# Attention by token tiles of eight heads, two tiles ahead, the product with the values 512 columns wide; the column of a mask constant inside an older tile

## The chip, the cores and the metric

The kernel runs on one core of a Trainium2 chip (trn2). The time is the device time of one execution in microseconds. The core has a matrix engine (TensorE, PE in the profile, with its weight loads as PEld), a vector engine (VectorE, DVE), a scalar engine for activations and copies (ScalarE, ACT), a general engine (GpSimd, POOL) and a sync engine that starts most transfers (SyncE, SP). They run side by side, each through its own queue of instructions in a fixed order, and wait for one another by semaphores. On-chip memory has 128 partitions; results of matmuls land in PSUM, which has eight banks of 2 KB for each partition.

## The reference

One decoder block over 1024 tokens of width 1024, all in float32. What matters here is the attention: eight query heads of 64, two key/value heads, each token sees itself and the 127 tokens before it, and each head has a sink in its softmax.

```python
h = _rmsnorm(x, g_mix_pre[l])
proj = jnp.einsum('bsd,de->bse', h, w_in[l]) + b_in[l]
u_pool, q, k, v, gates = jnp.split(proj, IN_SPLITS, axis=-1)
...
q = _partial_rotary(q.reshape(B, S, N_Q_HEADS, HEAD_DIM), cos, sin)
k = _partial_rotary(k.reshape(B, S, N_KV_HEADS, HEAD_DIM), cos, sin)
...
# in _sliding_window_sink_attention, over blocks of 128 tokens and the block before each
s = jnp.einsum('bnqhgd,bnkhd->bnhgqk', qb, kk).astype(jnp.float32) * scale
rel = qi + BLOCK - kj
band = (rel >= 0) & (rel < WINDOW)
s = jnp.where(valid[None, :, None, None], s, NEG_INF)
p = jax.nn.softmax(jnp.concatenate([s, sink], axis=-1), axis=-1)[..., :-1]
o = jnp.einsum('bnhgqk,bnkhd->bnqhgd', p.astype(v.dtype), vv)
```

Beside it stands a multi-scale pooling branch on the first 512 columns of `proj` (window sums of 2, 4, 8 and 16 tokens, less the token itself). Gates, an output projection and an MLP follow.

## The kernel before

Every matmul operand is split into a high part of reduced precision and a low part, what is left of it (`split`: ACT copies the high part, L103, DVE subtracts, L106). A product is then three matmuls: high by high, high by low, low by high (`PASSES`).

The stages are: projections of queries, keys and values of the first four token tiles while weights and input arrive; the attention stage; the pooling branch and the gates; the merge of both branches; the MLP. The change lies in the attention stage, from about 54 to 180 us of the profile. The stages behind it have the same instructions in the same order before and after.

In the attention stage the order of TensorE's instructions is written out by hand (`tc.manual_schedule` for PE). The order on the other engines is set by the scheduler of the language. Two streams are interleaved on TensorE:

- `others()`, a generator of filling work: the query products (`mm_q`, L182, 512 columns) and key/value products (`mm_kv`, L191, 256 columns) of tiles 4 to 7, each followed by `pre_qkv(n)`, and then the products of the pooling branch's input for its four groups (L533), each scaled by DVE (L536). `fill(t)` takes about t microseconds of it by a planned cost of each piece.
- attention itself, by half-tiles (n, g): token tile n of 128 queries, and four of its eight heads, a group g.

The steps of attention:

- `pre_qkv(n)`: DVE takes queries, keys and values from PSUM, scales them and adds the bias (L261, L262); POOL (DVE for tile 0) rotates.
- `post_qkv(n)`: TensorE transposes queries and keys (L279, L280), ACT and DVE split them into `qt`, `khi` and `klo`; POOL prepares the values `v` and the difference `dv` to the tile before (L286 to L296).
- `score(n, g)`: twelve matmuls (L321) into `sc`, which has a single buffer of two PSUM banks; ACT copies the own block to `s4` (L324); DVE overwrites by a mask with scores of the block before (`copy_predicated`, L326), then the maximum (L329) and the softmax bias (L330). After masking each query has 128 scores in one row: the own block up to the diagonal and the block before past it.
- `attend_t(n, g)`: the sink term (L340, L341), four exponentials with their sums on ACT (L344), sum, reciprocal and scaling on DVE (L345 to L347), four transposes on TensorE (L350) into an `at` bank, the split, and for n > 0 a masked copy of both parts, `pc` (L357).
- `attend_v(n, g)`: the product with the values, matmuls of 256 columns (L367), twelve for a half-tile and six for those of tile 0; ACT copies the result to `y` (L370).

In the loop over the 16 half-tiles, `attend_t` of one half-tile, a fill of 1.6, the score three half-tiles ahead, `post_qkv` two tiles ahead in every other step, a fill of 2.2, and `attend_v` follow each other. Once four tiles are done, SP sends `y` to memory (L579), and its place serves the window sums of `pool_in` (L595, L598) on DVE. These are followed by `pool_mix` (L611 to L613, L614) and the gates (L458).

PSUM is used as: `sc` one buffer of two banks, `at` three banks, `mm` three banks. The buffers named below are in the pool `ap`: `qkv` 4 of 4 KB for each partition, `sc4` 4 of 2 KB, `s4` 4 of 4 KB.

Of the kernel before, what the change touches and what calls it, by code (L numbers as in the profile page):

```python
# [14 lines left out]
P = 128  # L15
# [11 lines left out]
F = 4096  # L27
NF = F // P
HEAD_ORDER = (0, 4, 1, 5, 2, 6, 3, 7)

SOFT_ORDER = (0, 1, 4, 5, 2, 3, 6, 7)


PASSES = ((0, 0), (0, 1), (1, 0))
# [18 lines left out]
def block_kernel(ctx: ExitStack, tc, xt, x, consts, vecs, sinks, b_qkv, g_post, g_mlp, g_mlp_post,  # L53
# [100 lines left out]
    eps = cp.tile([P, 1], F32, name="eps")  # L154
    dve.memset(eps, EPS)
    pad = sp.tile([P, 32], F32, name="pad", bufs=1)
    dve.memset(pad, 0.0)
    warm = small(1, "warm")
    act.activation(warm, eps, AF.Identity)
    ident = cst[:, C_ID:C_ID + P]  # L160
# [1 line left out]

    from_prev = cst[:, C_MASK:C_MASK + P].bitcast(mybir.dt.uint32)
    own_t = cst[:, C_MASK + P:C_MASK + 2 * P]
    neg = cp.tile([P, 1], F32, name="neg")
    dve.memset(neg, NEG)

    def bcast(src, n):
        t = bcp.tile([P, 1024], F32, tag="bc", name=nm("bc"))
# [29 lines left out]
    sq = at("qkv", 4, [S])  # L199
    ones = vec[:, V_ONE:V_ONE + 1]  # L200
    for k in range(NK):
        xs = at("s4", 4, [S])
# [51 lines left out]
    tfs = {}  # L254

    def pre_qkv(n):
        tf = y[1][n - 2].rearrange("p a b -> p (a b)") if n in (2, 3) else at("qkv", 4, [1024])
        tfs[n] = tf
        t = tf[:, :768].rearrange("p (h d) -> p h d", d=HD)
        rn = r1[:, n:n + 1]  # L260
        dve.scalar_tensor_tensor(tf[:, :512], bq[n], rn, bq_b[:, :512], ALU.mult, ALU.add)  # L261
        dve.scalar_tensor_tensor(tf[:, 512:768], bkv_of(n), rn, bq_b[:, 512:768], ALU.mult, ALU.add)  # L262
        c = cst[:, C_COS + 8 * n:C_COS + 8 * n + 8].unsqueeze(1).unsqueeze(1).broadcast_to([P, 10, 2, 8])
        s = cst[:, C_SIN + 8 * n:C_SIN + 8 * n + 8].unsqueeze(1).unsqueeze(1).broadcast_to([P, 10, 2, 8])
        rot = t[:, :10, :ROT].rearrange("p h (a b) -> p h a b", a=2)
# [6 lines left out]
        eng.tensor_tensor(rot[:, :, 1, :], a[:, :, 1, :], b[:, :, 0, :], ALU.add)  # L272

    def post_qkv(n):
        tf = tfs[n]
# [9 lines left out]
        vt = at("v", 4, [2, 3, HD], F32R)  # L285
        pool.memset(f32(vt[:, :, 1, :]), 0.0)  # L286
        split(vt[:, 0, ::2, :], vt[:, 1, ::2, :], t[:, 10:12, :], pool, pool)
        vs[n] = vt.rearrange("p l a d -> p l (a d)")
        qts[n] = qt
        if n:  # L290

            dt_ = at("dv", 3, [2, 3, HD], F32R)
            dv = tf[:, 768:896].rearrange("p (a d) -> p a d", d=HD)
            pool.tensor_tensor(dv, t[:, 10:12, :], tfs.pop(n - 1)[:, 640:768].rearrange("p (a d) -> p a d", d=HD),
                               ALU.subtract)
            pool.memset(f32(dt_[:, :, 1, :]), 0.0)  # L296
            split(dt_[:, 0, ::2, :], dt_[:, 1, ::2, :], dv, pool, pool)
            dvs[n] = dt_.rearrange("p l a d -> p l (a d)")

    scores, soft = {}, {}  # L300

    SCALE = HD ** -0.5

    def score(n, g):


        qt = qts[n]
        k0 = max(n - 1, 0) * P
        nk = 2 * P if n else P
        s4 = at("sc4", 4, [4, P])  # L310
        if g == 0:
            soft[n] = tuple(sp.tile([P, NH], F32, tag=t, name=nm(t)) for t in ("nmx", "es", "den"))
        nmx = soft[n][0]
        sb = bank("sc", [2, 2, 256])

        for i in range(2):
            m = 2 * g + i
            for j, (qx, kx) in enumerate(((0, klo), (1, khi), (0, khi))):
                for kv in range(2):
                    r = slice(kv * HD, (kv + 1) * HD)  # L320
                    pe.matmul(sb[:, kv, i, :nk], qt[r, qx, m * P:(m + 1) * P], kx[r, k0:k0 + nk],  # L321
                              start=j == 0, stop=j == 2)
        heads = sb.rearrange("p a b k -> p (a b) k")
        act.copy(s4, heads[:, :, nk - P:nk])  # L324
        prev = heads[:, :, :P] if n else neg.unsqueeze(1).broadcast_to([P, 4, P])
        dve.copy_predicated(s4, from_prev.unsqueeze(1).broadcast_to([P, 4, P]), prev)  # L326

        gs = slice(4 * g, 4 * g + 4)
        dve.tensor_reduce(nmx[:, gs], s4, AX.X, ALU.max)  # L329
        dve.scalar_tensor_tensor(nmx[:, gs], nmx[:, gs], -SCALE, nsnk[:, gs], ALU.mult, ALU.min)  # L330
        scores[n, g] = s4

    probs = {}

    def attend_t(n, g):

        s4 = scores.pop((n, g))
        nmx, es, den = soft[n]
        gs = slice(4 * g, 4 * g + 4)
        dve.tensor_tensor(es[:, gs], snk[:, gs], nmx[:, gs], ALU.add)  # L340
        act.activation(es[:, gs], es[:, gs], AF.Exp)  # L341
        for j in range(4):
            h = 4 * g + j
            act.activation(s4[:, j], s4[:, j], AF.Exp, scale=SCALE, bias=nmx[:, h:h + 1], accum_out=den[:, h:h + 1])  # L344
        dve.tensor_tensor(den[:, gs], den[:, gs], es[:, gs], ALU.add)  # L345
        dve.reciprocal(den[:, gs], den[:, gs])
        dve.tensor_tensor(s4, s4, den[:, gs].unsqueeze(2).broadcast_to([P, 4, P]), ALU.mult)  # L347
        b = bank("at", [4, P])
        for j in range(4):
            pe.transpose(b[:, j], s4[:, j], ident)  # L350
        pt = at("s4", 4, [2, 4, P], F32R)
        split(pt[:, 0], pt[:, 1], b)
# [7 lines left out]
    def attend_v(n, g):  # L360
        pt, pc = probs.pop((n, g))
        yb = bank("at", [2, P])
        parts = ((vs[n - 1], pt), (dvs[n], pc)) if n else ((vs[0], pt),)
        mms = [(v, p, kv, j) for v, p in parts for kv in range(2) for j in PASSES]
        mms.sort(key=lambda e: (e[1] is pc, e[3][1]))
        for j, (v, p, kv, (vh, ph)) in enumerate(mms):
            pe.matmul(yb.rearrange("p m q -> p (m q)"), v[:, vh, kv * HD:kv * HD + P],  # L367
                      p[:, ph, 2 * kv:2 * kv + 2].rearrange("p i q -> p (i q)"), start=j == 0, stop=j == len(mms) - 1)
# [139 lines left out]
        return ga_.tile([P] + shape, F32R, tag="ga", name=nm("ar"))  # L508

    def others():  # L510
        for n in range(4, NT):
            bq[n] = bank("mm")
            for k in range(NK):
                mm_q(n, k, bq[n])
                yield 3 * 0.227
            if n == NT - 1:
                wu[3] = load_w(w_u[3], [NK, P])
            bkv[n] = bank("at" if n == 4 else "mm", [1, 256])
            for k in range(NK):
                mm_kv(n, k)  # L520
                yield 3 * 0.12
            pre_qkv(n)
        for gi in (3, 2, 1, 0):
            if gi:
                wu[gi - 1] = load_w(w_u[gi - 1], [NK, P])
# [23 lines left out]
                return  # L549
            owed[0] -= c  # L550

    half_steps = [(n, g) for n in range(NT) for g in range(2)]
    with tc.manual_schedule(engines={mybir.EngineType.PE}):
        pre_qkv(0)
        pre_qkv(1)
        pre_qkv(2)
        pre_qkv(3)
# [639 lines left out]
def _layout(inputs):  # L1197
# [18 lines left out]
    for col, t in ((C_COS, np.cos(ang)), (C_SIN, np.sin(ang))):  # L1216
# [48 lines left out]
```

## Time and profile before

| What | Value |
|---|---|
| median of 3 runs | 1159.61 us (1158.52 to 1160.14) |
| the profiled execution, its time | 1159.59 us |
| its span in the profile | 1157.8 us |
| busy PE, DVE, ACT, POOL, 54 to 180 us | 123.27, 107.68, 70.40, 23.72 us of 126 |
| last product with the values begins | 176.71 us |
| first gate matmul begins | 184.09 us |
| mean granted clock of TensorE | 0.993 |

The profile is one execution. The span reaches from the first to the last recorded instruction; the time holds the 1.8 us around it as well. An instruction's length in a timeline is its own; instructions that follow each other without a wait overlap a little, so that the distance between two starts is shorter (a sum over 512 columns on DVE is 0.69 long and its successor starts 0.60 later). The granted clock is the share of full speed that TensorE was given.

### The profile page before, as it was taken

The page shows a single profiled execution, that of the slowest core. Times are in us where ns is not written, and L with a number is a line of the kernel's source. Part 1 is how long each engine was busy: PE and PEld are TensorE (multiplying, and loading weights), DVE is VectorE, ACT ScalarE, POOL GpSimd, SP SyncE. Part 2 cuts the span into 40 slices and gives each one's busy share as a digit, 9 for nine tenths or more (in the row PEclk, how much of TensorE's full clock was granted, in tenths as well). Part 3 has the DMA queues.
Part 4 walks back from the last instruction along what each step waited for, and adds up shares of the span by engine and source line. Part 5 has one row for each costly group of instructions (what it writes and reads, how often), then busy time and mean ns, then how long its engine had stood idle before and what let it go on. Part 6 is the DMA issues. An engine that isn't in the chain of part 4 may idle for free.

```text
span 1157.8 us, 14205 instructions
## 1 busy us (share of the span) xinstructions
PE 1135.5 (98%) x5292; PEld 932.2 (81%) x5292; DVE 825.8 (71%) x1272; ACT 526.1 (45%) x920; POOL 62.9 (5%) x102
## 2 busy tenths in 40 slices
PE   7999999899999999999999999999999999999997
PEld 6888887788888888888788888888888888888885
DVE  7678997987654584766997766666547945446887
ACT  6455547443431334365654444444444345344342
POOL 3522100000000150000000000000000000000000
PEclk9999998999999999999999999999999999999999
DMA  7202107553345453433265434343688665432662
GB/s 253 81 1 64 56 19 273 177 169 128 143 171 179 149 177 109 134 131 119 91 218 218 156 144 160 141 159 141 249 286 301 211 214 170 132 101 73 201 198 92
DMA packets 66165, 179.08 MB, mean 155 GB/s; under 512 B 6192, under 2 KB 6192, under 8 KB 66096
## 3 DMA queue, kind: packets, MB, share of 16 engines
q1 hardware_dynamic: 60336, 157.73, 40.3%
q10 hardware_dynamic: 5760, 20.45, 4.4%
q8 instruction: 41, 0.67, 0.2%
q14 instruction: 28, 0.23, 0.1%
HBM read 127.82 MB, written 50.33 MB: 154 GB/s over the span
## 4 chain that ended last, share of the span: by engine, by line
PE 85%; DVE 9%; ACT 3%; issue 2%; DMA 1%; SPq 0%; DVEq 0%; ACTq 0%
PE mm L458 22%; PE at L458 16%; PE at L1103 14%; PE mm L1103 11%; PE mm L820 7%; PE mm L395 5%; PE mm L397 3%; PE mm L182 2%; PE mm L533 1%; PE at L820 1%; DVE s L357 1%; DVE wh L106 1%; DVE T L106 1%; DVE t L595 1%; DVE s L106 1%
## 5 line engine op out<-in xcount | busy, mean ns | idle before, releaser
L1103 PE MATMUL at<-ar,wh 128*128 128x512 f32 x744 | 169.6, 389 | 0.0
L1103 PEld LDWEIGHTS at<-ar,wh 128*128 128x128 f32 x744 | 139.6, 188 | 29.4 <-DVE ar L106 0.4
L1103 PE MATMUL mm<-ar,wh 128*128 128x512 f32 x576 | 131.0, 389 | 0.0
L1103 PEld LDWEIGHTS mm<-ar,wh 128*128 128x128 f32 x576 | 108.1, 188 | 22.4
L103 ACT CAST wh<-st 128x512 fp32r<-128x512 f32 (+1 forms) x106 | 66.9, 641 | 126.5 <-PE mm L395 36.6
L106 DVE TENSOR_TENSOR wh<-raw,wh 128x1024 fp32r<-128x1024 f32 x53 | 64.8, 1223 | 81.9 <-ACT wh L103 81.8
L103 ACT CAST wh<-raw 128x1024 fp32r<-128x1024 f32 x53 | 55.8, 1053 | 132.8 <-PE at L1103 63.6
L106 DVE TENSOR_TENSOR wh<-st,wh 128x512 fp32r<-128x512 f32 (+1 forms) x106 | 82.9, 788 | 17.9 <-ACT wh L103 15.7
L458 PE MATMUL mm<-gr,wh 128*128 128x512 f32 x300 | 72.7, 392 | 0.1
L458 PE MATMUL mm<-T,wx 128*128 128x512 f32 x288 | 68.0, 391 | 0.0
L458 PEld LDWEIGHTS mm<-gr,wh 128*128 128x128 f32 x300 | 56.0, 188 | 12.3 <-ACT g L885 0.5
L458 PEld LDWEIGHTS mm<-T,wx 128*128 128x128 f32 x288 | 54.1, 188 | 11.7
L458 PE MATMUL at<-T,wx 128*128 128x512 f32 x252 | 59.5, 391 | 0.0
L458 PE MATMUL mm<-x,wh 128*128 128x512 f32 x216 | 55.7, 415 | 3.4 <-ACT g L465 3.4
L458 PEld LDWEIGHTS at<-T,wx 128*128 128x128 f32 x252 | 47.3, 188 | 10.2
L458 PEld LDWEIGHTS mm<-x,wh 128*128 128x128 f32 x216 | 43.2, 200 | 14.5 <-ACT g L465 3.8
L106 DVE TENSOR_TENSOR ar<-B,ar 128x1024 fp32r<-128x1024 f32 x37 | 45.1, 1218 | 8.9 <-ACT ar L103 8.9
L533 PE MATMUL mm<-x,wh 128*128 128x512 f32 x192 | 49.9, 404 | 0.0
L458 PE MATMUL at<-gr,wh 128*128 128x512 f32 x183 | 44.5, 390 | 0.0
L103 ACT CAST ar<-B 128x1024 fp32r<-128x1024 f32 x37 | 38.7, 1046 | 10.7 <-DMA B<-in_w_dn_dram 6.1
L737 DVE TENSOR_TENSOR g<-g,mm 128x512 f32<-128x512 f32 x32 | 20.5, 683 | 31.2 <-PE mm L397 31.1
L533 PEld LDWEIGHTS mm<-x,wh 128*128 128x128 f32 x192 | 34.5, 188 | 7.4
(356 smaller groups left out, 2231.1 us busy)
## 6 DMA issues: line engine op xcount, KB each, us to landing
raw<-f_dram SPq DMA_DIRECT2D x53, 512.0 KB, 3.7
f_dram<-g SPq DMA_DIRECT2D x30, 512.0 KB, 3.2
B<-in_w_dn_dram SPq DMA_DIRECT2D x24, 512.0 KB, 6.1
st<-in_w_up_dram SPq DMA_DIRECT2D x22, 512.0 KB, 3.7
f_dram<-g ACTq DMA_DIRECT2D x17, 512.0 KB, 2.6
st<-in_w_g_dram SPq DMA_DIRECT2D x16, 512.0 KB, 3.7
g<-spill_dram SPq DMA_DIRECT2D x16, 512.0 KB, 4.5
raw<-in_w_dn_dram SPq DMA_DIRECT2D x16, 512.0 KB, 4.6
```

What stands on the lines that cost most here:

```text
L103: act.copy(hi, src)
L106: eng.tensor_tensor(lo, src, f32(hi), ALU.subtract)
L182: pe.matmul(bq, xs_[k][n // 4][:, xh, n % 4 * P:(n % 4 + 1) * P], wq[k][:, h, :], start=k == 0 and j == 0, stop=k == NK - 1 and j == 2)
L357: dve.tensor_tensor(pc[:, h], f32(pt[:, h]), own_t.unsqueeze(1).broadcast_to([P, 4, P]), ALU.mult)
L395: pe.matmul(bs[th], whi[:, k, :], rhs(k, hl, th), start=k == 0 and hl == 0, stop=False)
L397: pe.matmul(bs[th], wlo[:, k, :], rhs(k, 0, th), start=False, stop=k == nk - 1)
L458: pe.matmul(b, w[:, wh, kt, :], xo[kt][:, xh, :], start=not after and kt == 0 and j == 0, stop=kt == 3 and j == 2, skip_group_check=after)
L533: pe.matmul(b, (whi, wlo)[h][:, k, :], xr(k, xh, th), start=k == 0 and j == 0, stop=k == NK - 1 and j == 2)
L595: dve.tensor_tensor(t[:, step:], src[:, step:], src[:, :S - step], ALU.add)
L737: dve.tensor_tensor(z[:, sl], z[:, sl], bs[th], ALU.mult)
L820: pe.matmul(obs[n][dj], l, wos[k][whl][:, dj * 512:(dj + 1) * 512], start=k == 0 and hl == 0 and whl == 0, stop=k == NK - 1 and hl == 1)
L1103: pe.matmul(bs[t], fo[fh][:, k2, t * P:(t + 1) * P], wo_[wh][:, k2, :], start=not after and s2 == 0 and k2 == 0 and j == 0, stop=s2 == NS ...
```

## The change

Attention is done by whole tiles of eight heads.

- Both scores of a tile write halves of one buffer `s8` (three buffers of 4 KB). Maximum, softmax bias, sink term, sum, reciprocal and scaling are done once for eight heads, in a new function `softmax(n)`, which is called right after the tile's second score, two tiles ahead of its use.
- `attend_t(n)` is now the transposes of eight heads into two `at` banks, their splits, and the masked copies at width 1024. The high and low parts are separate `s4` tiles, so that one token tile takes all four buffers.
- `attend_v(n)` makes matmuls of 512 columns, twelve for a tile and six for tile 0, into one bank; ACT copies it in two pieces.
- The loop runs over eight tiles. The fills are 2.5, 2.0 and 2.5, with the two scores of tile n + 2 on either side of the middle one, and `post_qkv` three tiles ahead.
- The filling work makes both query products of tiles 6 and 7 before their key/value products.
- `post_qkv` first copies the values to a tile of their own (`vf`) on POOL; `qkv` has three buffers rather than four.
- The constant for masked scores, `neg`, is a column of the padding tile `pad`, which is now filled with it.
- The sinks are in the order of heads, as the softmax now is.

```diff
-    dve.memset(pad, 0.0)
+    dve.memset(pad, NEG)
...
-    neg = cp.tile([P, 1], F32, name="neg")
-    dve.memset(neg, NEG)
+    neg = pad[:, :1]
...
-        tf = y[1][n - 2].rearrange("p a b -> p (a b)") if n in (2, 3) else at("qkv", 4, [1024])
+        tf = y[1][n - 2].rearrange("p a b -> p (a b)") if n in (2, 3) else at("qkv", 3, [1024])
...
+    def split_v(src, tag, bufs):
+        t = at(tag, bufs, [2, 3, HD], F32R)
+        pool.memset(f32(t[:, :, 1, :]), 0.0)
+        split(t[:, 0, ::2, :], t[:, 1, ::2, :], src, pool, pool)
+        return t.rearrange("p l a d -> p l (a d)")
...
+        vf = at("vf", 3, [2, HD])
+        pool.tensor_copy(vf, t[:, 10:12, :])
+        vfs[n] = vf
+        vs[n] = split_v(vf, "v", 4)
         if n:
-
-            dt_ = at("dv", 3, [2, 3, HD], F32R)
...
+            dv = at("df", 1, [2, HD])
+            pool.tensor_tensor(dv, vf, vfs.pop(n - 1), ALU.subtract)
+            dvs[n] = split_v(dv, "dv", 3)
...
-        s4 = at("sc4", 4, [4, P])
         if g == 0:
-            soft[n] = tuple(sp.tile([P, NH], F32, tag=t, name=nm(t)) for t in ("nmx", "es", "den"))
-        nmx = soft[n][0]
+            scores[n] = at("s8", 3, [2, 4, P])
+        s4 = scores[n][:, :, 2 * g:2 * g + 2, :]
         sb = bank("sc", [2, 2, 256])
...
+        act.copy(s4, sb[:, :, :, nk - P:nk])
+        dve.copy_predicated(s4, wide(from_prev), sb[:, :, :, :P] if n else wide(neg))
+
+    soft = {}
+
+    def softmax(n):
+
+        s8 = scores[n].rearrange("p a b k -> p (a b) k")
+        nmx, es, den = (sp.tile([P, NH], F32, tag=t, name=nm(t)) for t in ("nmx", "es", "den"))
+
+        dve.tensor_reduce(nmx, s8, AX.X, ALU.max)
+        dve.scalar_tensor_tensor(nmx, nmx, -SCALE, nsnk, ALU.mult, ALU.min)
+        dve.tensor_tensor(es, snk, nmx, ALU.add)
+        act.activation(es, es, AF.Exp)
+        for h in range(NH):
+            act.activation(s8[:, h], s8[:, h], AF.Exp, scale=SCALE, bias=nmx[:, h:h + 1], accum_out=den[:, h:h + 1])
+        dve.tensor_tensor(den, den, es, ALU.add)
+        dve.reciprocal(den, den)
+        dve.tensor_tensor(s8, s8, den.unsqueeze(2).broadcast_to([P, NH, P]), ALU.mult)
...
+    def attend_t(n):
+
+        s8 = scores.pop(n)
+        pt = [at("s4", 4, [NH, P], F32R) for _ in range(2)]
+        for kv in range(2):
+            b = bank("at", [4, P])
+            for m in range(4):
+                pe.transpose(b[:, m], s8[:, kv, m], ident)
+            split(*(t[:, 4 * kv:4 * kv + 4] for t in pt), b)
         pc = None
         if n:
-            pc = at("s4", 4, [2, 4, P], F32R)
-            for h in range(2):
-                dve.tensor_tensor(pc[:, h], f32(pt[:, h]), own_t.unsqueeze(1).broadcast_to([P, 4, P]), ALU.mult)
-        probs[n, g] = pt, pc
+            pc = [at("s4", 4, [NH, P], F32R) for _ in range(2)]
+            for t, s in zip(pc, pt):
+                dve.tensor_tensor(t, f32(s), own_t.unsqueeze(1).broadcast_to([P, NH, P]), ALU.mult)
+        probs[n] = pt, pc
+
+    def attend_v(n):
+        pt, pc = probs.pop(n)
+        yb = bank("at", [4, P])
+        mms = [(v, p, kv, j) for v, p in (((vs[n - 1], pt), (dvs[n], pc)) if n else ((vs[0], pt),))
+               for j in ((0, 0), (1, 0), (0, 1)) for kv in range(2)]
         for j, (v, p, kv, (vh, ph)) in enumerate(mms):
             pe.matmul(yb.rearrange("p m q -> p (m q)"), v[:, vh, kv * HD:kv * HD + P],
-                      p[:, ph, 2 * kv:2 * kv + 2].rearrange("p i q -> p (i q)"), start=j == 0, stop=j == len(mms) - 1)
+                      p[ph][:, 4 * kv:4 * kv + 4].rearrange("p i q -> p (i q)"), start=j == 0, stop=j == len(mms) - 1)
         c = (n % 4) * P
-        act.copy(y[n // 4][g][:, :, c:c + P], yb)
+        for g in range(2):
+            act.copy(y[n // 4][g][:, :, c:c + P], yb[:, 2 * g:2 * g + 2])
...
     def others():
-        for n in range(4, NT):
-            bq[n] = bank("mm")
...
+        for qs, kvs in (((4,), (4,)), ((5,), (5,)), ((6, 7), (6, 7))):
+            for n in qs:
+                bq[n] = bank("mm")
...
         fill(8.3)
         post_qkv(0)
         make_rb()
         score(0, 0)
-        fill(2.0)
+        fill(2.5)
         post_qkv(1)
         score(0, 1)
-        fill(4.0)
+        softmax(0)
+        fill(3.0)
         score(1, 0)
-        fill(3.0)
-        for i, (n, g) in enumerate(half_steps):
-            attend_t(n, g)
-            fill(1.6)
-            if i + 3 < len(half_steps):
-                score(*half_steps[i + 3])
-            if g == 0 and n + 2 < NT:
-                post_qkv(n + 2)
-            fill(2.2)
-            attend_v(n, g)
-            if n % 4 == 3 and g == 1:
+        fill(2.5)
+        post_qkv(2)
+        score(1, 1)
+        softmax(1)
+        fill(5.5)
+        for n in range(NT):
+            attend_t(n)
+            fill(2.5)
+            if n + 2 < NT:
+                score(n + 2, 0)
+            fill(2.0)
+            if n + 2 < NT:
+                score(n + 2, 1)
+                softmax(n + 2)
+            if n + 3 < NT:
+                post_qkv(n + 3)
+            fill(2.5)
+            attend_v(n)
+            if n % 4 == 3:
...
-        ("sinks", c(a["attn_sinks"][0][list(SOFT_ORDER)])),
+        ("sinks", c(a["attn_sinks"][0])),
```

More of the change, by code (lines that the diff above doesn't have):

```diff
@@ L198, in block_kernel @@
     bss = bank("at", [NT])
-    sq = at("qkv", 4, [S])
+    sq = at("qkv", 3, [S])
     ones = vec[:, V_ONE:V_ONE + 1]
@@ L272, in pre_qkv @@
         eng.tensor_tensor(rot[:, :, 1, :], a[:, :, 1, :], b[:, :, 0, :], ALU.add)
+    vfs = {}
+    def split_v(src, tag, bufs):
[3 more added lines that the diff above has]
+        return t.rearrange("p l a d -> p l (a d)")
     def post_qkv(n):
-        tf = tfs[n]
+        tf = tfs.pop(n)
         t = tf[:, :768].rearrange("p (h d) -> p h d", d=HD)
@@ L284, in post_qkv, with wide @@
         split(khi[:, ks], klo[:, ks], bk[:, :P])
[L285 to L288, printed above, removed]
         qts[n] = qt
+        vf = at("vf", 3, [2, HD])
+        pool.tensor_copy(vf, t[:, 10:12, :])
+        vfs[n] = vf
+        vs[n] = split_v(vf, "v", 4)
         if n:
-            dt_ = at("dv", 3, [2, 3, HD], F32R)
[L293 to L300, printed above, removed]
+            dv = at("df", 1, [2, HD])
+            pool.tensor_tensor(dv, vf, vfs.pop(n - 1), ALU.subtract)
+            dvs[n] = split_v(dv, "dv", 3)
+    scores = {}
     SCALE = HD ** -0.5
+    def wide(ap):
+        return ap.unsqueeze(1).unsqueeze(1).broadcast_to([P, 2, 2, P])
     def score(n, g):
@@ L322, in score @@
                               start=j == 0, stop=j == 2)
[L323 to L330, printed above, removed]
@@ L331, in score @@
-        scores[n, g] = s4
-    probs = {}
[L335 to L352, printed above, removed]
+        act.copy(s4, sb[:, :, :, nk - P:nk])
@@ L358, in attend_t @@
-        probs[n, g] = pt, pc
[L360 to L365, printed above, removed]
+            pc = [at("s4", 4, [NH, P], F32R) for _ in range(2)]
+            for t, s in zip(pc, pt):
+                dve.tensor_tensor(t, f32(s), own_t.unsqueeze(1).broadcast_to([P, NH, P]), ALU.mult)
@@ L510, in others @@
     def others():
-        for n in range(4, NT):
-            bq[n] = bank("mm")
-            for k in range(NK):
-                mm_q(n, k, bq[n])
-                yield 3 * 0.227
+        for qs, kvs in (((4,), (4,)), ((5,), (5,)), ((6, 7), (6, 7))):
+            for n in qs:
+                bq[n] = bank("mm")
+                for k in range(NK):
+                    mm_q(n, k, bq[n])
+                    yield 3 * 0.227
             if n == NT - 1:
                 wu[3] = load_w(w_u[3], [NK, P])
[L518 to L522, printed above, removed]
+            for n in kvs:
+                bkv[n] = bank("at" if n == 4 else "mm", [1, 256])
+                for k in range(NK):
+                    mm_kv(n, k)
+                    yield 3 * 0.12
+                pre_qkv(n)
         for gi in (3, 2, 1, 0):
@@ L550, in fill @@
             owed[0] -= c
-    half_steps = [(n, g) for n in range(NT) for g in range(2)]
     with tc.manual_schedule(engines={mybir.EngineType.PE}):
[L554 to L557, printed above, removed]
+        for n in range(4):
+            pre_qkv(n)
         fill(8.3)
```

1 line of the change is left out of this document (removed).

## The prediction

> **What bounds the kernel now.** I read the page first: the span, the busy shares and the chain that ended last.
>
> ```profile
> span 1157.8 us, 14205 instructions
> PE 1135.5 (98%) x5292; PEld 932.2 (81%) x5292; DVE 825.8 (71%) x1272; ACT 526.1 (45%) x920; POOL 62.9 (5%) x102
> ...
> PE 85%; DVE 9%; ACT 3%; issue 2%; DMA 1%; SPq 0%; DVEq 0%; ACTq 0%
> ```
>
> TensorE carries 85% of the chain: time is gained or lost where it stands still or runs at a lower clock. Then busy time by stage (columns: stretch, its length, busy us and instructions of PE, PEld, DVE, ACT, POOL, granted clock, DMA share, GB/s). The attention stage, which the change rewrites, is the second row.
>
> ```profile
> 40.00:54.00 14.00, 13.86 (x78) 11.96 (x77) 8.18 (x20) 4.10 (x5) 5.68 (x15) 0.88 0.11 40
> 54.00:180.00 126.00, 123.27 (x831) 104.29 (x829) 107.68 (x229) 70.40 (x229) 23.72 (x59) 1.00 0.14 46
> 180.00:240.00 60.00, 55.22 (x217) 43.77 (x218) 51.03 (x80) 35.90 (x55) 0.00 (x0) 0.91 0.60 208
> ```
>
> In attention PE is busy for 123.3 of 126 us, DVE for 107.7. Then what PE waited for from 54 to 184 us (in total, times, longest):
>
> ```profile
> PE at L611 <- ACT ar L103: 1.9, 1, 1.9
> PE at L350 <- DVE qt L106: 1.1, 2, 0.9
> PE sc L321 <- DVE klo L106: 0.6, 1, 0.6
> PE at L612 <- DVE ar L106: 0.6, 1, 0.6
> ```
>
> Only 1.7 us of PE waits lie inside attention (L350, L321); the other two come after it. Last, PE's timeline at the stage's end:
>
> ```profile
> 176.71 0.88 PE L367 MATMUL at<-s,dv 128*128 128x256 f32 x6
> 177.43 0.40 PE L611 MATMUL at<-ar,wpt 128*128 128x512 f32 x1
> ...
> 180.85 0.79 PE L611 MATMUL at<-ar,wpt 128*128 128x512 f32 x2 [1.87 <-ACT ar L103]
> 182.22 0.79 PE L612 MATMUL at<-ar,wpt 128*128 128x512 f32 x1 [0.57 <-DVE ar L106]
> ...
> 184.09 7.62 PE L458 MATMUL mm<-x,wh 128*128 128x512 f32 x24
> ```
>
> Attention ends at 177.4, the gates begin at 184.1. After a gap of 1.87 and one of 0.57 us the 24 matmuls take 7.46 us start to start (184.09 to 191.55), where 24 at full clock take 5.5 (0.229 each, from nine at 0.228 to eighteen at 0.238). The granted clock reads 0.50 from 182 to 188 us.
>
> **The change, part by part.** It keeps all matmul work but for the product with the values.
>
> *PE.* 180 matmuls of 256 columns become 90 of 512. Six of 256 follow each other in 0.715 us (88.20 to 88.91), 0.119 each: 21.4 us. A 512 takes 0.229: 90 make 20.6. Gain 0.85. Each tile now has one run of transposes and one of the product instead of two; with the boundaries of such runs costing 0.1 to 0.2 (nine matmuls before a score 2.27, before a product 2.18, alone 2.06) that is about 1.0 over eight tiles. If nothing waits, the 1.1 us before L350 go too. Gain in all: 2.95.
>
> *DVE.* Per tile, one set of the small operations goes: L330 0.16, L340 0.20, L345 0.17, L346 0.17, and some 0.06 on each of four pairs fused to width 1024: 0.9, in eight tiles 7 us. That shortens a queue; what it does to PE depends on order, below.
>
> *ACT* loses eight L341 (0.2 each); *POOL* gains eight copies of the values (0.29 to 0.59, the L105 and L106 rows), 2 to 5 us on an engine busy 24 of 126; *the mask column* in the padding tile removes one memset while DVE waits for the first input; the order of sinks is the host's; the key/value product of tile 7 comes later and its query product earlier, with every bank read before its next use in the planned order. All zero. Their cover is slack of several us; without it POOL's longest copy, 0.6, would be the cost. *SP* sends the two y stores of the first half only after tile 3's product, some 14 us later than now (120.3), and the first window sum (L595) waits for their landing (4.9 us): about 141 by the layout below, where DVE reaches it at 140.6. Cost 0.4 on DVE, off PE's path.
>
> *The new waits.* There is one pair of score banks. Before, the two scores of a tile stood some 7 us apart, with half-tile softmax between. Now the second score comes after nine matmuls of fill (2.1 us). It needs the mask copy (copy_predicated) of the first done. In the built program DVE's queue holds ahead of that copy: sum, reciprocal and scaling of the previous tile's softmax, which wait for eight exponentials, then two low-part casts and two products with the mask at width 1024. Behind the waiting sum stand all of these, and PE waits for the last.
>
> Prices: mask copy 0.73; low cast 0.60 and query cast on ACT 0.57 (pitch); one exponential with its read 0.39 (61.00, 61.38, 61.77), eight with es 3.4; score copy on ACT 0.58; small operations 0.15 to 0.18. Width 1024 of the mask product and scaling: 1.13 to 1.21 (L595, L106 wh); I take 1.15 and 1.2. A maximum over 1024 stands nowhere: between 0.69 (one of 512) and 1.38 (two); I take 1.25, near the 1024-wide sums.
>
> First place (A), tile 0: the fill ahead of score(0,1) is three matmuls longer, so it ends at 61.7 (now 61.0). ACT copy to 62.3, mask copy behind the query and key casts to 63.2, maximum to 64.4, bias 64.6, exponentials to 68.0, sum and reciprocal 68.4, scaling 69.7 (with hand-offs), mask copy of score(1,0) 70.4. PE: 12 matmuls and three narrow to 64.9, score(1,0) 65.85, 21 narrow 68.35, transposes 68.85. **Stall 1.6**.
>
> Laid on: score(1,1) 71.4, 24 matmuls 77.0, transposes of tile 0 77.7, 12 matmuls 80.5, score(2,0), nine matmuls 83.6, score(2,1) 84.55 without a wait (mask copy 83.5). DVE then has a weight split (1.15), mask copy 85.95, maximum 87.75, bias 88.2; ACT's exponentials of tile 2 run to 91.6, y copies to 92.3, casts of tile 1 92.9 and 93.4; DVE scaling 93.2, low casts 94.45, mask products 96.75, mask copy of score(3,0) 97.45. PE reaches score(3,1) at 94.4. Second place (B): **stall 3.05**.
>
> From there the ring per tile on DVE is: mask copy 0.75, query cast 0.6, maximum 1.25, key cast and bias 0.4, exponentials 3.4, sum to scaling 1.6, low casts 1.25, mask products 2.3, mask copy 0.75, u 0.6: 12.9, with hand-offs 13.2, and 1.0 more when DVE waits for the second score's copy (score 0.95, copy 0.6, less u). Weight splits (1.15) and the window sums of two groups come on top in tiles 5 to 7. PE's tile: transposes 0.7, 31 fill matmuls 7.1, two scores 1.8, query transposes 0.5, product 2.75, boundaries 0.6: 13.5. So they are nearly level, DVE mostly behind: the same laying on gives stalls of 1.2 (score(5,1)), 0.3 (score(6,1)), 2.9 (score(7,1), behind four window sums and two splits) and 0.5 at the product of tile 6. Bounds for these four: 0 to 10 (1.5 to 2 in each of five tiles); I take 4.9.
>
> *Clock.* At 180.85 it fell after gaps of 1.87 and 0.57, at 215.5 after one of 3.35; not after 0.89 (147.68). Around 216 the clock reads 0.88, 0.50 and 0.77 over three stretches of 2 us: 3.4 us at half, which costs PE 1.7. I expect it after B and the stall of 2.9, part of it in the shade of DVE's lag: 1.5, bounds 0 and 5.
>
> [...]
>
> After attention PE waits for the last window casts as now, behind the same DVE work; the order of instructions from the gates on is unchanged. I take the delay as carried whole; the 3.35 us gap before 214.69 could hide at most that much.
>
> **Sum.** -2.95 + 1.6 + 3.05 + 4.9 + 1.5 = +8.1 us. The profiled execution took 1159.59 (span 1157.8 and 1.8 around), the median is 1159.61: 1167.7.
>
> **Rivals.**
> - *PE stays the bound* (faster): the mask copy is done before each second score. It decides if DVE runs 1.6 us earlier at A and 3.05 at B than laid out. For it: 7 us less DVE work, PE saturated now, DVE often 20% free. Against: DVE's order puts a wait for exponentials of 3.4 us once in each tile. 1159.6 - 2.95 = 1156.6.
> - *Stalls and gains cancel*: A and half of B alone, 3.1 against 2.95: 1159.8. For it: the later tiles are near level.
> - *DVE's ring binds every tile*, each stall followed by half clock: A, B, 10 and 5, less 2.95: +16.7, 1176. For it: DVE is busy 20.0 of 20 us from 140 to 160 now, when the window sums begin.
> - *The clock holds through every stall here*: 1167.7 - 1.5 = 1166.2. Against it the 0.50 after the gap of 1.87. [...]
> - *The wide product isn't quicker*, if bound by weight loads: only 0.85 worse; inside the forecast.
>
> **How the numbers follow.** Forecast 0.50 (1163 to 1172), clock holds 0.10 (1162 to 1171), ring binds throughout 0.14 (1172 to 1180), cancel 0.10, PE the bound 0.16 (1155.5 to 1157.3). A measurement tells 0.2%, 2.3 us, from no change. Slower 0.50 + 0.10 + 0.14 = 0.74, same 0.10, faster 0.16. The range 1157 to 1175 leaves out most of the fastest case and the upper half of the ring: about 0.2. The forecast's own range is 1163 to 1172.
>
> **What would show it.** PE idle before the second score of a tile, with the mask copy of the first (copy_predicated) as releaser: about 1.6 near 69 us and 3 near 95. The last product with the values ending near 186 instead of 177.6, the first 24 gate matmuls near 192 instead of 184.1. Granted clock 0.5 for some 3 us within attention. DVE's busy time down by some 7 us. Wrong would be: no wait at the second scores, or waits of PE for other tiles (casts, window sums); then the layout of DVE's queue fails. If the stage ends at 186 and the time is unchanged, the carrying fails.

## The result, and the profile after

| | changed kernel | kernel before, beside it |
|---|---|---|
| median | 1154.52 us (12 runs, 1152.36 to 1158.48) | 1159.51 us (12 runs, 1157.82 to 1162.86) |
| ratio | 0.996, 95% interval 0.9948 to 0.9973 | |
| profiled execution, its time | 1154.03 us | 1159.59 us |
| first score of attention to first gate matmul | 132.46 us (54.48 to 186.94) | 127.53 us (56.56 to 184.09) |
| first gate matmul to the end of the span | 965.3 us | 973.7 us |

The kernel is faster by 0.4%, where slower by 0.7% was forecast. The last two rows hold the riddle. Attention did become longer, by 4.9 us. Everything behind it, whose instructions and their order on TensorE are the same in both kernels, became shorter by 8.4 us, and of that the prediction says nothing.

The page of the changed kernel: the span, the busy shares, the chain that ended last.

```profile
span 1152.2 us, 13954 instructions
PE 1120.7 (97%) x5202; PEld 925.8 (80%) x5202; DVE 820.4 (71%) x1209; ACT 525.1 (46%) x912; POOL 70.0 (6%) x110
PE 85%; DVE 9%; ACT 3%; DMA 2%; issue 1%; SPq 0%; DVEq 0%
```

TensorE still carries the chain, and it is busy for 14.8 us less. Busy time by stage in the changed kernel (same columns as before):

```profile
54.00:180.00 126.00, 117.81 (x710) 97.00 (x711) 98.52 (x159) 65.44 (x214) 29.57 (x63) 0.99 0.09 32
180.00:240.00 60.00, 52.25 (x218) 41.56 (x217) 51.66 (x82) 35.76 (x58) 0.00 (x0) 0.97 0.63 228
```

In the stretch of attention TensorE is busy for 5.5 us less. Its waits stand where they were forecast: TensorE's timeline in attention, the lines with a wait in front (in brackets: idle before, releaser; L326 is the mask copy).

```profile
68.47 0.39 PE L323 MATMUL sc<-klo,qt 64*128 64x256 f32 x2 [1.30 <-DVE s L326]
95.75 0.39 PE L323 MATMUL sc<-klo,qt 64*128 64x256 f32 x2 [2.40 <-DVE s L326]
125.54 0.39 PE L323 MATMUL sc<-klo,qt 64*128 64x256 f32 x2 [1.06 <-DVE s L326]
139.07 0.39 PE L323 MATMUL sc<-klo,qt 64*128 64x256 f32 x2 [0.28 <-DVE s L326]
155.68 0.39 PE L323 MATMUL sc<-klo,qt 64*128 64x256 f32 x2 [2.66 <-DVE s L326]
```

The stage's end in the same timeline; compare the last line with 7.62 us for the same 24 matmuls before, which began at half clock (0.50 granted from 181.38 to 188.20 us).

```profile
180.26 1.52 PE L369 MATMUL at<-s,dv 128*128 128x512 f32 x6
...
184.24 0.73 PE L622 MATMUL at<-ar,wpt 128*128 128x512 f32 x2 [1.09 <-ACT ar L101]
185.93 0.50 PE L623 MATMUL at<-ar,wpt 128*128 128x512 f32 x1 [0.95 <-DVE ar L104]
...
186.94 5.60 PE L461 MATMUL mm<-x,wh 128*128 128x512 f32 x24
```

Where do the 8.4 us come from? With each matmul of the changed kernel set beside the same one of the kernel before, the changed kernel is 2.9 us behind at the first gate matmul and 2.9 at 238 us: in between, what the kernel before loses at half clock is offset by a wait of 2.22 us in the changed kernel (196.63, for the last window casts). From there on its place doesn't jump anywhere: level at 388, 2.7 us ahead at 494, 4.3 at 719, 5.3 at 822, 5.6 at 900, and constant from there. So matmuls themselves are quicker, a little each. TensorE's timeline, kernel before:

```profile
243.97 2.21 PE L458 MATMUL mm<-gr,wh 128*128 128x512 f32 x9
...
246.72 2.96 PE L458 MATMUL mm<-x,wh 128*128 128x512 f32 x12
```

and the same twelve matmuls in the changed kernel:

```profile
249.53 2.88 PE L461 MATMUL mm<-x,wh 128*128 128x512 f32 x12
```

One matmul is some 0.39 long, and eleven starts lie between the first and the last of twelve: (2.96 - 0.40) / 11 = 233 ns from start to start before, (2.88 - 0.39) / 11 = 226 after. The line above it, with the same shape and other operands, had (2.21 - 0.40) / 8 = 226 in the kernel before too. The granted clock was 1.00 at all three.

What tells the quick from the slow ones is where the operands lie. The kernel's on-chip memory is filled from two sides. Weight pieces (`wh`), `gr` and the attention tiles are in pools that grow from the left; `x` and the sums `T` of the MLP are in pools on the right. Matmuls whose operands lie on the same side take 227 ns; those with one on each side took 233 before and take 227 now. The diff touches this at one place: `neg` was a tile of its own, 32 bytes for each partition, in a pool at the left end. Without it every later left-hand pool starts 32 bytes lower (`wh` at 24032 rather than 24064), and the right-hand ones stay (`x` at 147424). The distance between the sides was 32 bytes modulo 512, and is 0.

### The profile page after: what moved, and what is told of

It reads as the page before. It is cut to its first block, busy times and chain, and to the rows that moved or that the text cites. A ratio compares the mean times of both kernels' runs of the same rounds, so it can differ in the third digit from the quotient of the medians.

```text
span 1152.2 us, 13954 instructions
## 1 busy us (share of the span) xinstructions
PE 1120.7 (97%) x5202; PEld 925.8 (80%) x5202; DVE 820.4 (71%) x1209; ACT 525.1 (46%) x912; POOL 70.0 (6%) x110
## 4 chain that ended last, share of the span: by engine, by line
PE 85%; DVE 9%; ACT 3%; DMA 2%; issue 1%; SPq 0%; DVEq 0%
PE mm L461 20%; PE at L461 16%; PE at L1114 14%; PE mm L1114 11%; PE mm L831 5%; PE mm L398 5%; PE mm L179 3%; PE mm L400 3%; PE at L188 1%; PE sc L179 1%; DVE s L360 1%; ACT s L340 1%; PE at L831 1%; PE mm L538 1%; PE sc L323 1%
## 5 line engine op out<-in xcount | busy, mean ns | idle before, releaser
L101 ACT CAST wh<-st 128x512 fp32r<-128x512 f32 (+1 forms) x106 | 67.0, 642 | 123.7 <-PE mm L398 34.1
L104 DVE TENSOR_TENSOR wh<-raw,wh 128x1024 fp32r<-128x1024 f32 x53 | 64.8, 1223 | 80.9 <-ACT wh L101 80.5
L101 ACT CAST wh<-raw 128x1024 fp32r<-128x1024 f32 x53 | 55.8, 1053 | 131.1 <-PE at L1114 62.6
L104 DVE TENSOR_TENSOR wh<-st,wh 128x512 fp32r<-128x512 f32 (+1 forms) x106 | 82.9, 788 | 16.4 <-ACT wh L101 14.0
L461 PE MATMUL mm<-x,wh 128*128 128x512 f32 x216 | 52.5, 399 | 3.5 <-ACT g L468 3.5
L104 DVE TENSOR_TENSOR ar<-B,ar 128x1024 fp32r<-128x1024 f32 x37 | 45.0, 1217 | 9.4 <-ACT ar L101 9.4
L538 PE MATMUL mm<-x,wh 128*128 128x512 f32 x192 | 48.7, 404 | 0.0
L101 ACT CAST ar<-B 128x1024 fp32r<-128x1024 f32 x37 | 38.8, 1050 | 11.1 <-DMA B<-in_w_dn_dram 6.2
```

Source lines behind the costliest of these rows:

```text
L101: act.copy(hi, src)
L104: eng.tensor_tensor(lo, src, f32(hi), ALU.subtract)
L461: pe.matmul(b, w[:, wh, kt, :], xo[kt][:, xh, :], start=not after and kt == 0 and j == 0, stop=kt == 3 and j == 2, skip_group_check=after)
L538: pe.matmul(b, (whi, wlo)[h][:, k, :], xr(k, xh, th), start=k == 0 and j == 0, stop=k == NK - 1 and j == 2)
```

## The experiments

Two theories for the 8.4 us. *Placement*: the distance between the operands of a matmul sets its pitch, and the attention rewrite by itself is a loss. Its rival: the gain is the rewrite's, and the pitch follows from something else that it changed (other engines' traffic, or the clock). What the rewrite did in attention comes after that.

### One part alone

**e1**: the kernel before, with the constant in the padding tile and nothing else of the change.

```diff
-    dve.memset(pad, 0.0)
+    dve.memset(pad, NEG)
-    neg = cp.tile([P, 1], F32, name="neg")
-    dve.memset(neg, NEG)
+    neg = pad[:, :1]
```

> The kernel before with one edit: the mask constant is a column of the padding tile, so that one tile of 32 bytes for each partition goes and every buffer on the left side of the on-chip memory moves down by 32 bytes. Theory P (placement): matmuls with one operand on the left side and one on the right side follow each other at 227 ns instead of 234; some 8.5 us of the changed kernel's profile is this, so 1159.5 falls to about 1151, and the attention stage keeps its form. Theory R (the pitch belongs to a chip or a run, not to the program): 1159.5, pitch 234. Theory A (the gain comes from the attention by whole tiles): 1159.5.

Measured: 1149.57 us (1149.11 to 1151.58), before 1158.92; ratio 0.9918 (0.9905 to 0.9932). One line is worth 9.5 us by the ratio. The line of e1 that answers to the twelve matmuls above:

```profile
245.41 2.88 PE L457 MATMUL mm<-x,wh 128*128 128x512 f32 x12
```

**e2**: the changed kernel, with these lines taken back.

> The changed kernel with the mask constant in a tile of its own again, as before; attention stays by whole tiles. Theory P: the left side moves back up by 32 bytes, pitch 234 returns, 1154.5 rises by about 8 to 1162 or 1163: the attention rewrite alone is slower than the kernel before by 2 to 4 us, for its waits at the second scores (7.7 us in the profile). Theories R and A: 1154.5.

Measured: 1164.92 us (1164.41 to 1169.2); ratio 1.0054 (1.0038 to 1.0069). The rewrite of attention without the column is a loss of 6 us, where 2 to 4 were expected. Its timeline has the waits of the changed kernel (7.3 us at the second scores) and the old pitch:

```profile
252.20 2.96 PE L462 MATMUL mm<-x,wh 128*128 128x512 f32 x12
```

The rival falls: the gain comes without the rewrite and goes with the column.

### What about the placement counts

A dummy tile put first on the right side moves all right-hand pools and leaves the left-hand ones. Its width is the only thing that differs:

```diff
+    rpad = ctx.enter_context(tc.tile_pool(name="rpad", bufs=1, side="right"))
+    rtile = rpad.tile([P, 8], F32, name="rtile")
...
+    dve.memset(rtile, 0.0)
```

**e3**, 32 bytes (8 columns) in the kernel before:

> The kernel before, its mask column untouched, with a dummy tile of 32 bytes opened first on the right side, so that the right side moves down by 32 bytes and the left stays. Theory P in its relative form (both sides have to stand at the same place within 64 bytes): both at 0, pitch 227, about 1151. In its absolute form (the left side has to stand at 32): pitch 234, 1159.5. Theory R: 1159.5.

**e5**, the same 32 bytes in the changed kernel:

> The changed kernel with a tile of 32 bytes for each partition put first on the right side of on-chip memory, so that the right-hand pools move 32 bytes and lose the offset to the left-hand ones that the change had given them (left less right: 0 modulo 512 bytes in the changed kernel, 32 here). Relative theory (the matmuls are quick when both operands stand alike to each other): mixed pairs go back to 233 to 235 ns and the time to 1163 to 1165 us. Absolute theory (quick when the left-hand pools start 32 bytes past a multiple of 64, wherever the right-hand ones are): 227 ns and 1154 to 1155 us.

**e6**, 480 bytes (120 columns) in the kernel before:

> The kernel before with a tile of 480 bytes for each partition put first on the right side, so that right-hand pools start at multiples of 512 bytes as the left-hand ones do (left less right 0 modulo 512), and neg stays in its own tile. Relative theory: 227 ns for mixed pairs and 1149 to 1150 us, as with the mask column in the padding tile. Absolute theory (left at 32 past a multiple of 64): 234 ns and 1159 us.

**e7**, 96 bytes (24 columns) in the kernel before:

> The kernel before with a tile of 96 bytes put first on the right side: left less right is 128 bytes modulo 512. Relative theory with a period of 64 or 128 bytes: 227 ns and 1149 to 1150 us; with a period of 256 or 512 bytes: 234 ns and 1159 us, or a pitch of its own in between. Absolute theory: 234 ns and 1159 us.

**e9**, 224 bytes (56 columns) in the kernel before:

> The kernel before with a tile of 224 bytes put first on the right side: the two sides then stand 256 bytes apart modulo 512. If what counts is the distance modulo 256, matmuls of 512 columns with one operand on each side take 227 ns and the kernel 1149 to 1150 us; if modulo 512, 232 to 234 ns and 1158 to 1159 us.

Measured, sorted by distance (starts of the large left-hand and right-hand tiles modulo 512 bytes; mean ns from start to start of neighbouring matmuls of 512 columns, steps over 300 ns left out, for the some 1,700 steps in which this matmul's streamed operand and the next one's weights lie on different sides, and the some 2,700 in which they lie on one). The kernel before was at 1157.98 to 1159.51 us beside these runs, so times are best compared by the ratios:

| Kernel | left, right | distance | different sides | one side | time, ratio (interval) |
|---|---|---|---|---|---|
| changed | 480, 480 | 0 | 227.3 | 226.8 | 1154.52, 0.996 (0.9948 to 0.9973) |
| e1 | 480, 480 | 0 | 227.6 | 226.8 | 1149.57, 0.9918 (0.9905 to 0.9932) |
| e6 | 0, 0 | 0 | 227.5 | 226.7 | 1149.12, 0.9926 (0.9912 to 0.9939) |
| before | 0, 480 | 32 | 233.3 | 227.2 | 1159.51, 1 |
| e2 | 0, 480 | 32 | 233.3 | 227.2 | 1164.92, 1.0054 (1.0038 to 1.0069) |
| e5 | 480, 448 | 32 | 233.3 | 227.3 | 1165.03, 1.0058 (1.0046 to 1.0071) |
| e3 | 0, 448 | 64 | 232.7 | 227.5 | 1159.54, 1.0005 (0.9992 to 1.0019) |
| e7 | 0, 384 | 128 | 232.7 | 227.4 | 1157.98, 0.9999 (0.999 to 1.0007) |
| e9 | 0, 256 | 256 | 227.5 | 226.7 | 1149.01, 0.9921 (0.9907 to 0.9935) |

The gain vanishes in the changed kernel when the right side is moved by 32 bytes (e5), and appears in the kernel before when the right side is moved to match (e6), with `neg` where it was. So it is the distance: the left side's own start (0 or 480) makes no difference, and the memset that the change saved isn't it either. 64 and 128 bytes are as bad as 32, 256 as good as 0: of the five distances that were tried, 0 and 256 are quick (227.3 to 227.6 ns) and 32, 64 and 128 are not (232.7 to 233.3 ns). "Alike modulo 64", which e3 was expected to bear out at 1151 us, fell with e3, "alike modulo 128" with e7 and "alike modulo 512" with e9. The line of e9 that answers to the two above:

```profile
247.06 2.88 PE L461 MATMUL mm<-x,wh 128*128 128x512 f32 x12
```

The size fits. Kernel before: 1,693 steps at 233.3 - 227.6 = 5.7 ns are 9.7 us, and 2,700 at 227.2 - 226.7 are 1.3 us more: 11.0 us if every one stood on the path. By the ratios 8.6 (e6), 9.2 (e9) and 9.5 us (e1) were measured in the kernel before, and 10.9 (e2) and 11.4 (e5) in the changed kernel, which has some 1,770 such steps.

### What attention lost, and whether it had to

DVE's timeline in the changed kernel around the second stall (PE waits from 93.35 to 95.75 for the mask copy at 94.99):

```profile
86.28 0.17 DVE L337 TENSOR_TENSOR es<-snk,nmx 128x8 f32<-128x8 f32 x1
89.42 0.48 DVE L259 SCALAR_TENSOR_TENSOR qkv<-mm,r,bc 128x256 f32<-128x256 f32 x1 [2.98 <-PE mm L188]
89.82 0.16 DVE L341 TENSOR_TENSOR den<-den,es 128x8 f32<-128x8 f32 x1
90.01 0.20 DVE L342 RECIPROCAL den<-den 128x8 f32<-128x8 f32 x1
90.25 1.34 DVE L343 TENSOR_TENSOR s<-s,den 128x1024 f32<-128x1024 f32 x1
91.52 1.27 DVE L104 TENSOR_TENSOR s<-at,s 128x512 fp32r<-128x512 f32 x2
92.71 2.35 DVE L360 TENSOR_TENSOR s<-s,cst 128x1024 fp32r<-128x1024 f32 x2
94.99 0.71 DVE L326 COPY_PREDICATED s<-cst,sc 128x512 f32<-128x512 uint32 x1
```

This is the queue of the prediction, in its order: scaling, low casts and the products with the mask all stand ahead of the copy that TensorE needs. The score itself was done at 91.4.

**e4**: other fills.

```diff
-        fill(2.5)
+        fill(4.0)
...
-        fill(5.5)
+        fill(4.0)
         for n in range(NT):
             attend_t(n)
-            fill(2.5)
+            fill(4.5)
...
-            fill(2.0)
+            fill(2.5)
...
-            fill(2.5)
             attend_v(n)
```

> The changed kernel with the fill around the scores moved: 4.5 before the first score of a tile, 2.5 between the scores, none before the product with the values (was 2.5, 2.0, 2.5), and ahead of the loop 4.0 and 4.0 instead of 2.5 and 5.5. Theory W (the 7.7 us of waits at the second scores are paid in full, since the mask copy lies late in the queue of VectorE): waits at L323 fall to 2 or less, 1154.5 falls to 1147 to 1150. Theory D (the queue of VectorE sets the period of a tile anyway): the waits move to the transposes or the product with the values, 1153 or more.

Measured: 1154.69 us (1153.31 to 1156.55), ratio 0.9963 (0.995 to 0.9976): the same as the changed kernel. TensorE's waits from 54 to 190 us in e4 (in total, times, longest):

```profile
PE sc L323 <- DVE s L326: 2.3, 2, 1.4
PE sc L323 <- DVE t L609: 2.1, 1, 2.1
...
PE at L354 <- ACT y L373: 0.7, 1, 0.7
```

The waits ahead of scores fell from 7.7 to 4.4 us, and first score to first gate from 132.5 to 129.0. But from there to the end the profiled execution took 2.7 us longer, of which 1.7 is a half-clock period of 6.8 instead of 3.4 us near 215 us. Whether that belongs to the kernel or to the run, one execution doesn't tell. As the medians stand, fills don't help; that DVE's work sets the period, as this run seemed to say, did not survive the next three.

**e8**: sum, reciprocal and scaling taken out of `softmax(n)` into `scaled(n)`, which is called after `score(n + 1, 0)`, and tied to it:

```diff
+    def scaled(n):
+        s8, es, den = soft.pop(n)
+        if n + 1 < NT:
+            dve.scalar_tensor_tensor(es, scores[n + 1][:, 0, 0, :NH], 0.0, es, ALU.mult, ALU.add)
```

> The changed kernel with sum, reciprocal and scaling of a tile's softmax moved on DVE behind the mask copy of the next tile's first score (forced by one small operation for each tile, about 0.16 us, that reads a masked score times zero; the result is unchanged). Theory Q (DVE stands idle in its queue for the exponentials, 10.6 us of waits at the sum in attention, and this wait is what costs attention its 5 us): waits at the second scores fall from 7.7 to 2 us or less, and the time to 1148 to 1150 us. Theory D (DVE's work and other waits in its queue set the period): waits of TensorE appear elsewhere, 1153 us or more.

Measured: 1152.1 us (1151.44 to 1155.62), ratio 0.9952 (0.9939 to 0.9966). The median is 2.4 us below the changed kernel's, but the kernel before was lower beside it too (1157.98 against 1159.51): by the ratios (0.9952 against 0.996) 0.9 us are left, and the intervals overlap, so no gain in time is shown. At 1159.51 the ratio gives 1153.9, on theory D's side. Theory Q's order was there, its effect was not: TensorE's and DVE's waits from 54 to 184 us in e8.

```profile
PE sc L323 <- DVE s L326: 6.4, 6, 2.6
```

```profile
DVE s L104 <- ACT s L101: 10.3, 4, 3.7
```

DVE's wait for the exponentials at the sum (10.6 us in all) only became a wait at the low casts (L104) for ACT's high casts (L101), which stand behind the same exponentials on ACT. The casts and the products with the mask were still ahead of the mask copy.

**e10** adds that: `masked(n)`, the products with the mask, after the next first score, and tied to it. **e11** has `masked(n)` without `scaled(n)`.

```diff
+    def masked(n):
+            z = small()[:, :1]
+            if n + 2 < NT:
+                dve.tensor_scalar(z, scores[n + 2][:, 0, 0, :1], 0.0, 0.0, ALU.mult, ALU.add)
...
+                    dve.scalar_tensor_tensor(t, f32(s), z, o, ALU.add, ALU.mult)
```

> The changed kernel with the late softmax steps moved as in the run before it (e8) and the two products with the mask, 1024 wide, moved on DVE behind the mask copy of the next first score as well (forced by one small operation of a masked score times zero, added to their operand; the result is unchanged). Theory M (what still holds the mask copy back, 2.56 and 2.36 us before two second scores in e8, is these two products, 2.35 us a tile, ahead of it in the queue): waits at the second scores fall from 6.4 to 2 us or less, and the time from 1152.1 to 1148 to 1150 us. Theory D (DVE's and ACT's work for a tile set the pace, the order only moves the wait): waits appear elsewhere, 1151.5 us or more.

> The same with the two products with the mask moved alone, and sum, reciprocal and scaling emitted where the changed kernel has them (the queue then puts the scaling partly behind the next mask copy by itself). Theory M: waits at the second scores 4 us or less, 1150 to 1152.5 us. Theory D: 1153.5 us or more.

Measured: e10 1148.01 us (1147.53 to 1150.2), ratio 0.9917 (0.9904 to 0.993); e11 1151.06 us (1150.08 to 1152.15), ratio 0.9941 (0.9928 to 0.9954). DVE's timeline of e10 at the same place, and what TensorE waited for from 54 to 184 us:

```profile
91.41 1.29 DVE L104 TENSOR_TENSOR s<-at,s 128x512 fp32r<-128x512 f32 x2 [1.77 <-ACT s L101]
92.61 0.72 DVE L326 COPY_PREDICATED s<-cst,sc 128x512 f32<-128x512 uint32 x1
...
93.55 2.48 DVE L374 SCALAR_TENSOR_TENSOR s<-s,sm,cst 128x1024 fp32r<-128x1024 f32 x2
```

```profile
PE sc L323 <- DVE s L326: 2.1, 5, 0.9
```

The mask copy comes 2.4 us earlier, and the waits at the second scores fall to 2.1 us (3.6 in e11). By the ratios e10 is 5.0 us quicker than the changed kernel, with intervals that don't touch, and e11 2.2 us, with intervals that overlap a little; at 1159.51 the ratios give 1149.9 and 1152.7 us. Theory M holds in e10 and D falls there: DVE does two more small operations in most tiles, and the kernel is quicker. e11 lies just above the range of M by this measure (its median lies in it) and below that of D. By the ratios the two moves bring 0.9 and 2.2 us alone and 5.0 together. So the loss in attention was one of order in a queue, not of work.

First score to first gate, profiled executions: 127.5 before; 126.9 to 127.3 with the sides alike and the old attention (e1, e6, e9); 132.5 with the rewrite, 132.9 and 133.7 without the placement (e2, e5); 129.6 in e8, 127.1 in e11, 126.7 in e10. Beside e1 (0.9905 to 0.9932) and e9 (0.9907 to 0.9935), e10's 0.9904 to 0.993 shows no difference: the rewrite in its best order here costs nothing and gains nothing that was measured. What both share is the placement.

## Why the prediction was wrong

**The step that failed** is "the mask column in the padding tile removes one memset while DVE waits for the first input [...] All zero." It costed the instruction that went and not the tile. The 32 bytes moved every left-hand pool behind them, and that was worth -8.6 to -9.5 us in the kernel before and -10.9 to -11.4 in the changed one, more than all other terms together. The evidence was in the working: "24 at full clock take 5.5 (0.229 each, from nine at 0.228 to eighteen at 0.238)". That is a mean over two groups, 227 and 233, at one shape and full clock, and the spread was taken for noise.

**No change of matmul pitch behind attention** was forecast ("the order of instructions from the gates on is unchanged. I take the delay as carried whole"). The delay was carried, and stood against 8.4 us of gain over the next 640 us. In e2, which has the delay alone, the stretch from the gates to the end is 974.8 us against 973.7: carried whole, as said, to about 1 us.

**The sum for the rewrite** was +8.1 us. Alone it measured +6.0 (e2, interval 4.4 to 8.0 by the ratio on 1158.92) and +7.0 (e5, 5.3 to 8.2): the direction right, the size somewhat high. Its terms in the changed kernel:

- Stall A, at score(1,1): 1.6 forecast, 1.30 measured, at 68.5 us. Stall B, at score(3,1): 3.05 forecast, 2.40 measured. The cause as laid out, DVE's queue ahead of the mask copy; e10 removed that and the stalls went.
- The four later places: 4.9 forecast. Score(5,1) 1.06 (1.2), score(6,1) 0.28 (0.3), score(7,1) 2.66 (2.9); the fourth, 0.5 at the product of tile 6, did not come. 4.0 in all.
- The wide product: 0.85 forecast from 0.119 and 0.229. It takes 227 ns against two of 119 (means): 90 times 11 ns, 1.0 us. The rival that it is not quicker falls.
- The waits before L350 are gone (1.1), as taken. The gain from fewer boundaries was not measured by itself.
- Clock: 1.5 forecast after B and the last stall. One period came, after B, 3.4 us long, worth 1.7; after the 2.66 us at 155.68 none. The prediction's reading of the kernel before was not quite right: the half clock there began at 181.4 us, after the gap of 1.87 alone; the gap of 0.57 ended at 182.22, inside it.

Busy time and granted clock (third column from the right) of the changed kernel, in steps of 2 us around B:

```profile
94.00:96.00 2.00, 0.24 (x4) 0.25 (x6) 1.70 (x2) 0.00 (x0) 0.00 (x0) 1.00 0.00 0
96.00:98.00 2.00, 2.00 (x18) 1.77 (x17) 0.47 (x1) 0.59 (x1) 0.00 (x0) 0.61 0.00 0
98.00:100.00 2.00, 2.00 (x7) 1.57 (x7) 1.63 (x3) 0.75 (x2) 0.00 (x0) 0.54 0.00 0
```

Stalls and clock are 7.7 + 1.7 = 9.4 us of the changed kernel, and attention grew by 4.9: 4.5 us were gained against a forecast of 2.95. Not all of them are the rewrite's. In e2, without the placement, 7.3 + 1.7 - 5.4 = 3.6 are left. Another 0.9 are the clock at the stage's end: the last four matmuls ahead of the gates take 1.87 us in the kernel before, at half clock (182.22 to 184.09), and 1.01 in the changed one (185.93 to 186.94). That leaves some 2.7, near the forecast. DVE's busy time in the window of attention fell by 9.2 us where 7 were named, in a window that ends some 4 us earlier in the stage. In the times of the profiles the last product ended at 181.8 (186 forecast) and the gates began at 186.9 (192): the kernel before had been held up by 2.1 us ahead of its first score in its profiled execution, where 3.4 us at half clock fell at 44.8.

Of the rivals, *PE stays the bound* had the right sign by luck and the wrong reason: 7.7 us of waits were there. *The ring binds every tile*, *cancel* and *the clock holds* are not what the trace shows. No rival named a cause outside the attention stage.

## What to carry to other kernels

Here the tile that went moved every tile behind it on its side by 32 bytes: list the addresses of matmul operands before and after a change, and give a change of placement a term of its own. When groups of equal matmuls at equal clock differ in pitch within one profile (233 and 227 ns here), ask which operands they have before averaging; one dummy tile of 224 bytes was worth 0.8% here. A long wait in a queue is worth moving only as far as the instruction that another engine waits for: moving the wait alone gave 0.9 us by the ratios, which is within the noise, and moving what stood between it and the mask copy as well gave 5.0.

## What the runs showed of the hardware

- Matmuls of 512 columns in single-precision operands, each with weights of its own, started every 227.3 to 227.6 ns (means) where the streamed operand and the weights loaded beside it lay on different sides at distances of 0 and 256 bytes (changed kernel, e1, e6, e9), and every 232.7 to 233.3 ns at 32, 64 and 128 bytes (kernel before, e2, e5, e3, e7). Other distances were not tried, and why the pitch differs no run shows. Matmuls of 256 columns went the other way: the key and value products started every 117 ns in the kernel before (32 bytes) and every 120 ns in the changed one (0 bytes; medians).
- At the distances of 32, 64 and 128 bytes matmuls with both operands on one side were slower too: 227.2 to 227.5 ns in the mean, against 226.7 to 226.8 at 0 and 256. Why is open.
- In the profile of the kernel before the granted clock reads 0.50 for 3.41 us from 44.84, for 6.83 us from 181.38, for 3.41 us from 215.51, and from 1154.17 to the end of the span; in that of the changed kernel for 3.41 us from 96.43 and from 219.31, and from 1147.74 to the end. The starts at 181.38 and 215.51 lie 136.54 and 170.67 us after the first one, 40 and 50 times 3.41; the one at 219.31 lies 122.88 us after the first of its profile, 36 times 3.41.
- Idle time of TensorE in the 3.41 us ahead of these starts, the last of each profile left out: 0.14, 1.87 and 2.60 us in the kernel before, 2.40 and 1.95 us in the changed one. Of the 3.41 us before 96.43 some were worked: TensorE's last matmul ahead of the wait ended at 93.35. In the changed kernel 1.52 us of idle time between 212.48 and 215.90 had no half clock behind them (1.00 from 215.90 to 219.31). So idle time alone doesn't tell the cases apart: 0.14 us was followed by half clock, and 1.52 was not.
- The 2.40 us of waiting before 95.75 lay in one such stretch of 3.41 us, and half clock followed; the 2.66 before 155.68 fell into two, 1.45 us to 154.46 and 1.22 us behind it, and none followed (1.00 from 156 to 160 us); the 2.56 before the same score in e5 (154.84) fell into two as 0.88 and 1.68 (counted back from the half clock behind it), and half clock followed at 156.6 (0.64 from 156 to 158 us, 0.50 from 158 to 160).
